# Feed-forward up-projection with the weight columns moving through TensorE, its result turned by VectorE and DRAM, its operand sums on GpSimd

## The chip, the cores and the metric

The kernel runs on one core of a Trainium2 chip. The metric is device microseconds for one execution, as the median of several runs. A core has TensorE (matmuls, "PE" in the profile, with "PEld" for its weight loads), VectorE ("DVE"), ScalarE ("ACT"), GpSimd ("POOL") and SyncE ("SP", which here only issues DMAs). The engines work at the same time, each through its own instructions in order, and wait for one another by semaphores.

## The reference

One residual block on x of 512 tokens by 2048, all in float32:

```python
h = rmsnorm(x); proj = h @ w_in                  # q, k, v of 8 + 8 heads, and forget gates
mixed = concat(headnorm(stick_breaking(...)), headnorm(forgetting(...)))
x = x + mixed @ w_out                            # 2048 x 2048
h2 = rmsnorm(x)
u = relu(h2 @ w_up)                              # 2048 x 8192
x = x + (u * u) @ w_down                         # 8192 x 2048
y = rmsnorm(x)
```

The change is in `h2 @ w_up`, called the first feed-forward product below; `(u * u) @ w_down` is the second.

## The kernel before

**Precision.** Every float32 operand is split into a high and a low part (`split`, lines 58 to 65): ScalarE rounds the operand to the high part (line 60), VectorE subtracts that from the operand (line 61). Each product is then three matmuls, high by high, high by low and low by high (`mm3`, lines 92 to 95).

**Seven products in place of eight.** Both feed-forward products are done in two-by-two blocks by Winograd's form of Strassen's method. The tokens' side has quarters a11, a21, a12, a22 (two halves of the contraction by two halves of 256 tokens), the weights' side b11, b12, b21, b22. Seven products are formed from sums of quarters. The sums of the tokens' side for the first product, "forms" in the code, are made once (`a_form`, lines 443 to 456), split, and stay in SBUF as `F[p]` for p = 1 to 7. The sums of the weights' side are made as the weights arrive, in place: in `Unit.product` there are four VectorE instructions for a unit, of 1024 elements in each partition (lines 542, 544, 546, 548).

**The first product before.** The 8192 columns of `w_up` are worked through in 32 units of 256 columns (`Unit`, line 516). For a unit two tiles of 1 MB are loaded on SP's queue (line 530; the pool `rw` has five buffers), and seven products are made. A product splits one quarter of the weights (1024 elements per partition) into a buffer from a ring (`hi_lo`, lines 69 to 75: three pairs of buffers in the pool `w`, and one more pair in `hx` from the end of the first unit on), and then does 8 x 3 matmuls: the weights are stationary (128 by 128), 256 tokens of `F[p]` move. The result has hidden columns in the partitions and tokens along the free axis, which is how the second product wants it. PSUM banks A, B and C hold running sums; ScalarE copies A out at three of the products (line 557), VectorE adds it to B or C (lines 563, 565, 569), and ScalarE applies relu and square (lines 570, 571).

**Forms of the hidden layer.** After every second unit the quarters of the result are turned into the seven forms of the second product (`store_form`, lines 573 to 581): for four of the seven VectorE makes a sum (lines 449 to 455), ScalarE and VectorE split into a buffer `st` (the tag `wraw` of the pool `w`, three buffers shared with others), and SP writes it to DRAM as `ufd`. They are read back as `uf` in the second product (`second`, lines 616 to 644), where 512 columns of `w_down` move and the forms are stationary.

**Order.** The program is written in order of work; a list scheduler with a cost model orders the instructions of each engine, and on the chip each engine then runs its list in order. The last two products of a unit (`old`, p = 4 and 3) are written in between those of the next unit (line 678).

Of the kernel before, what the change touches and what calls it, by code (L numbers as in the profile page):

```python
# [8 lines left out]
F32 = mybir.dt.float32  # L9
# [5 lines left out]
P = 128  # L15
NT = 512
# [19 lines left out]
def block_kernel(ctx, tc, x, g_attn, w_in, b_f, g_out_sb, g_out_fox, w_out, g_mlp, w_up, w_down, g_final, y):  # L36
# [399 lines left out]
    sm = ctx.enter_context(tc.tile_pool(name="sm", bufs=2, reuse_waits="tile"))  # L436
    xp_cm = tc.tile_pool(name="xp", bufs=1, reuse_waits="tile")
    xp = xp_cm.__enter__()
    trp_cm = tc.tile_pool(name="tr1", bufs=4, space=PSUM, reuse_waits="tile")
# [3 lines left out]
    def a_form(p, c, out, s=None):  # L443


        a11, a21, a12, a22 = (c[:, :, i, j:j + 2 * P] for i in range(2) for j in (0, 2 * P))
        s = a22 if s is None else s
        if p == 5:
            dve.tensor_tensor(s, a21, a22, op=ALU.add)
        if p == 6:  # L450
            dve.tensor_tensor(s, s, a11, op=ALU.subtract)
        if p == 7:
            dve.tensor_tensor(a21, a11, a21, op=ALU.subtract)
        if p == 3:
            dve.tensor_tensor(a12, a12, s, op=ALU.subtract)
        split(*out, {1: a11, 2: a12, 5: s, 6: s, 4: a22, 7: a21, 3: a12}[p])
# [3 lines left out]
    for n in range(4):  # L460
        ns = slice(n * NT, (n + 1) * NT)
        ps = [acc.tile([P, NT], F32, tag="acc", name="acco") for _ in range(TB)]
        x2 = xp.tile([P, TB, NT], F32, tag="x2", name="x2")
        for k0 in range(0, 2 * NH, 2):
# [6 lines left out]
            if k0 == 4:  # L471
                sp.dma_start(x2, xq[:, :, ns])
# [6 lines left out]
        hr = xp.tile([P, 2, 2, NT], F32, tag="hr", name="hr")  # L479
        for i in range(4):  # L480
            tr = trp.tile([P, NT], F32, tag="tr", name="tr1")
            for t in range(TB):
                pe.transpose(tr[:, t * P:(t + 1) * P], x2[:, t, i * P:(i + 1) * P], ident)
# [3 lines left out]
        s12 = xp.tile([P, 2, 2 * P], F32, tag="s12", name="s12")  # L487
        for p in (1, 5, 6, 2, 7, 4, 3):
            if n == 3 and p == 4:
                break  # L490
            a_form(p, hr, [f[:, 2 * n:2 * n + 2, :] for f in F[p]], s12)
        for t in range(TB):
            junk = xp.tile([P, NT], F32, tag="junk", name="junk")
            act.activation(junk, x2[:, t, :], AF.Square, accum_out=ss2[:, t, n:n + 1])
# [8 lines left out]
    ups_cm = tc.tile_pool(name="ups", bufs=2, space=PSUM, reuse_waits="tile")  # L503
    ups = ups_cm.__enter__()
    mps_cm = tc.tile_pool(name="mps", bufs=1, space=PSUM, side="right", reuse_waits="tile")
    mps = mps_cm.__enter__()
    M1 = [mps.tile([P, 2, NT], F32, name="m1_0")]
# [8 lines left out]
    class Unit:  # L516
        def __init__(self, u):
            self.u = u
            cols = slice(2 * u * P, 2 * (u + 1) * P)
            rows_ = w_up.rearrange("(a i p) f -> i p a f", i=2, p=P)  # L520
            if u == 0:

                self.b = [[wp.tile([P, KC // 2, P], F32, tag="wraw", name="wq") for _ in range(2)] for _ in range(1)]
                for j in range(2):
                    sp.dma_start(self.b[0][j], rows_[0][:, :, j * P:(j + 1) * P])
            else:
                self.b = []
            for i in range(len(self.b), 2):
                raw = rw.tile([P, KC // 2, 2 * P], F32, tag="rw", name="wu")
                sp.dma_start(raw, rows_[i][:, :, cols])  # L530
                self.b.append([raw[:, :, j * P:(j + 1) * P] for j in range(2)])
            self.A, self.B, self.C = (ups.tile([P, NT], F32, tag=c, name=f"ps{c}")[:, :2 * P] for c in "abc")

        def product(self, p):
            if p == 2:
                if self.u % 2 == 0:
                    hidden[0] = sg[0].tile([P, 2, 2, NT], F32, tag="c", name="c", bufs=2)
                self.pair = hidden[0]
                self.c = hidden[0][:, self.u % 2]
            (b11, b12), (b21, b22) = self.b  # L540
            if p == 5:
                dve.tensor_tensor(b11, b12, b11, op=ALU.subtract)
            if p == 6:
                dve.tensor_tensor(b11, b22, b11, op=ALU.subtract)
            if p == 4:
                dve.tensor_tensor(b21, b21, b11, op=ALU.subtract)
            if p == 7:
                dve.tensor_tensor(b12, b22, b12, op=ALU.subtract)
            hi, lo = (w.rearrange("p (a b) -> p a b", b=P) for w in hi_lo(2 * NT))
            split(hi, lo, {1: b11, 2: b21, 5: b11, 6: b11, 4: b21, 7: b12, 3: b22}[p])  # L550
            ps = {1: self.A, 6: self.A, 7: self.A, 4: self.A, 2: self.B, 5: self.C, 3: self.C}[p]
            for a in range(KC // 2):
                mm3(ps, hi[:, a, :], lo[:, a, :], F[p][0][:, a, :], F[p][1][:, a, :], a == 0 and p in (1, 2, 5), a == KC // 2 - 1)
            t1, t2 = slice(0, 2 * P), slice(2 * P, NT)
            if p in (1, 6, 7):
                self.m = sm.tile([P, 2 * P], F32, tag="m6" if p == 6 else "m", name=f"s{p}", bufs=2 if p == 6 else 1)
                act.copy(self.m, self.A)  # L557
                if p == 6:
                    self.m6 = self.m
                if p == 1:  # L560
                    self.m1 = self.m
            if p == 7:
                dve.tensor_tensor(self.c[:, 1, t2], self.m, self.C, op=ALU.add)
            if p == 2:
                dve.tensor_tensor(self.c[:, 0, t1], self.m1, self.B, op=ALU.add)
            if p == 4:
                act.copy(self.c[:, 0, t2], self.A)
            if p == 3:
                dve.tensor_tensor(self.c[:, 1, t1], self.m6, self.C, op=ALU.add)
                act.activation(self.c, self.c, AF.Relu)  # L570
                act.activation(self.c, self.c, AF.Square)

    def store_form(p, c, u):
        st = wp.tile([P, 2, 2, 2 * P], F32R, tag="wraw", name="st")
        a_form(p, c, (st[:, 0], st[:, 1]))
# [7 lines left out]
    def store_last(u, h):  # L583
        st = wp.tile([P, 2, NT], F32R, tag="wraw", name="su")
        split(st[:, 0], st[:, 1], hidden[0][:, u, h])
# [5 lines left out]
    UF_AT = dict(zip(ORDER, (1, 5, 6, 2, 7, 4, 3)))  # L591
    SUM_AT = dict(zip(ORDER[1:], (1, 5, 6, 2, 7, 4)))
    QUADS = [[2, 3], [4, 7]]
    M, uf = {}, {}
# [4 lines left out]
    def load_uf(p, group):  # L599
        uf[p] = form.tile([P, 2, group[1], 2 * P], F32R, tag=f"fh{UF_AT[p]}", name=f"uf{p}")  # L600
# [15 lines left out]
    def second(p, b, db, n, first):  # L616
# [10 lines left out]
        ps = M1[db] if p == 1 else dps.tile([P, 2, NT], F32, tag="dps", name="accd")  # L627
# [39 lines left out]
    hidden = {}  # L667
    todo, sg = [], []
    old = None
    for u in range(NU + 1):  # L670
        new = Unit(u) if u < NU else None
        if u == NU - 1:
            for p in ORDER:
                load_uf(p, GROUPS[0])
# [178 lines left out]
```

## Time and profile before

| | us |
|---|---|
| median of 3 runs | 2097.75 (2096.9 to 2097.83) |
| profiled execution, its own time | 2099.45 |
| its span, first to last instruction | 2097.7 |
| first matmul of the first feed-forward product | 818.9 |
| its end | 1473.5 |
| first matmul of the closing part (`last_product`) | 2039.55 |

The granted TensorE clock of the profiled execution is 0.998 over the span. The profile lists each engine's busy time; a matmul's own duration includes its way through the array, during which the next one has already started, so TensorE's pace is read from the distance of the starts. A "chain of waits" row names who waited, at which line, for whom, and for how long. A "windows" row gives the busy time of each engine in a stretch, with the number of instructions in brackets. Queues ("SPq") are the instruction streams that issue DMAs.

### The profile page before, as it was taken

How to read it: one execution, taken by the hardware profiler on the slowest of the kernel's cores; microseconds unless marked ns; L12 is line 12 of the kernel's file. 1: busy time of each engine (PE TensorE's matmuls, PEld its weight loads, DVE VectorE, ACT ScalarE, POOL GpSimd, SP SyncE). 2: the span in 40 equal slices, each digit the busy share in tenths (PEclk: the TensorE clock that was granted, in tenths of full speed). 3: DMA queues.
4: the chain of work that ended last, by engine and by line, in shares of the span. 5: the costliest groups of instructions: out<-in, count | busy, mean ns of one | idle time of the engine just before them, and what ended most of it. 6: DMA issues, size and time to landing. Idle time of an engine off the chain costs nothing.

```text
span 2097.7 us, 29846 instructions
## 1 busy us (share of the span) xinstructions
PE 2076.2 (99%) x12084; PEld 1841.3 (88%) x12084; DVE 1571.3 (75%) x1744; ACT 1034.7 (49%) x1396; POOL 50.5 (2%) x75
## 2 busy tenths in 40 slices
PE   8999999999999999999999999999999999999998
PEld 8888888888898888999999999999888888888886
DVE  5454555665677667878888888888788988888886
ACT  5333333444455564555666666566744443333433
POOL 0000000000010000000000000000000000000003
PEclk9999999999999999999999999999999999999999
DMA  6323323323223444466566566657856664664732
GB/s 185 88 81 91 81 82 79 81 81 85 77 81 110 155 147 151 123 209 192 181 213 199 171 208 206 189 184 248 299 202 263 237 227 178 242 251 139 268 113 81
DMA packets 239930, 339.68 MB, mean 162 GB/s; under 512 B 7936, under 2 KB 154416, under 8 KB 233776
## 3 DMA queue, kind: packets, MB, share of 16 engines
q1 hardware_dynamic: 238832, 335.64, 48.9%
q8 instruction: 95, 1.56, 0.3%
q10 hardware_dynamic: 960, 2.13, 0.3%
q14 instruction: 43, 0.35, 0.1%
HBM read 272.20 MB, written 65.54 MB: 161 GB/s over the span
## 4 chain that ended last, share of the span: by engine, by line
PE 58%; DVE 1%; DMA 0%; issue 0%; ACT 0%; SPq 0%; ACTq 0%
PE accd L93 8%; PE accd L95 8%; PE accd L94 8%; PE psa L93 6%; PE psa L95 6%; PE psa L94 6%; PE psc L93 3%; PE psc L95 3%; PE psc L94 3%; PE psb L95 1%; PE psb L94 1%; PE psb L93 1%; PE m L95 1%; PE m L93 1%; PE m L94 1%; PE acce L93 1%
## 5 line engine op out<-in xcount | busy, mean ns | idle before, releaser
L60 ACT CAST wh<-wu 128x1024 fp32r<-128x1024 f32 x164 | 171.0, 1048 | 135.9 <-PE psa L94 53.6
L61 DVE TENSOR_TENSOR wl<-wu,wh 128x1024 fp32r<-128x1024 f32 x164 | 199.6, 1222 | 45.7 <-ACT wh L60 45.4
L61 DVE TENSOR_TENSOR wl<-wraw,wh 128x1024 fp32r<-128x1024 f32 (+2 forms) x133 | 158.2, 1190 | 85.0 <-ACT wh L60 84.5
L93 PE MATMUL psa<-fh,wh 128*128 128x256 f32 x776 | 220.3, 284 | 0.8 <-ACT s L557 0.7
L94 PE MATMUL psa<-fl,wh 128*128 128x256 f32 x776 | 220.0, 284 | 0.9 <-DVE fl L61 0.9
L95 PE MATMUL psa<-fh,wl 128*128 128x256 f32 x776 | 219.8, 283 | 0.0
L60 ACT CAST wh<-wd 128x1024 fp32r<-128x1024 f32 (+1 forms) x136 | 134.7, 999 | 170.3 <-PE accd L95 108.8
L60 ACT CAST wh<-wraw 128x1024 fp32r<-128x1024 f32 (+2 forms) x133 | 135.4, 1019 | 156.7 <-PE accq L94 70.2
L93 PE MATMUL accq<-hH,wh 128*128 128x512 f32 x512 | 200.9, 392 | 0.0
L95 PE MATMUL accq<-hH,wl 128*128 128x512 f32 x512 | 200.5, 392 | 0.0
L94 PE MATMUL accq<-hL,wh 128*128 128x512 f32 x512 | 200.4, 391 | 0.0
L61 DVE TENSOR_TENSOR wl<-wd,wh 128x1024 fp32r<-128x1024 f32 (+1 forms) x136 | 155.6, 1154 | 41.9 <-ACT wh L60 41.5
L93 PE MATMUL accd<-wh,uf 128*128 128x512 f32 x436 | 169.7, 389 | 1.0 <-issue 1.0
L95 PE MATMUL accd<-wh,uf 128*128 128x512 f32 x436 | 169.6, 389 | 0.0
L94 PE MATMUL accd<-wl,uf 128*128 128x512 f32 x436 | 169.6, 389 | 0.0
L60 ACT CAST wx<-wd 128x1024 fp32r<-128x1024 f32 (+1 forms) x88 | 87.5, 1000 | 130.0 <-PE accd L95 78.2
L93 PEld LDWEIGHTS psa<-fh,wh 128*128 128x128 f32 x776 | 149.4, 192 | 1.2 <-ACT s L557 0.9
L94 PEld LDWEIGHTS psa<-fl,wh 128*128 128x128 f32 x776 | 149.4, 192 | 1.2 <-DVE fl L61 1.1
L95 PEld LDWEIGHTS psa<-fh,wl 128*128 128x128 f32 x776 | 149.3, 192 | 0.0
L61 DVE TENSOR_TENSOR wx<-wd,wx 128x1024 fp32r<-128x1024 f32 (+1 forms) x88 | 100.8, 1153 | 23.3 <-ACT wx L60 22.9
L94 PEld LDWEIGHTS accq<-hL,wh 128*128 128x128 f32 x512 | 96.2, 188 | 19.9 <-issue 0.5
L93 PEld LDWEIGHTS accq<-hH,wh 128*128 128x128 f32 x512 | 96.2, 188 | 19.6 <-issue 0.7
(299 smaller groups left out, 5502.1 us busy)
## 6 DMA issues: line engine op xcount, KB each, us to landing
wu<-in_w_up_dram SPq DMA_DIRECT2D x63, 1024.0 KB, 6.4
ufd<-st SPq DMA_DIRECT2D x98, 512.0 KB, 6.9
wd<-in_w_down_dram SPq DMA_DIRECT2D x48, 1024.0 KB, 6.9
wraw<-in_w_in_dram SPq DMA_DIRECT2D x84, 512.0 KB, 3.8
uf<-ufd SPq DMA_DIRECT2D x42, 1024.0 KB, 6.5
wraw<-in_w_out_dram SPq DMA_DIRECT2D x32, 512.0 KB, 3.5
wd<-in_w_down_dram SPq DMA_DIRECT2D x16, 768.0 KB, 6.2
uf<-ufd SPq DMA_DIRECT2D x14, 768.0 KB, 6.0
```

The lines of the kernel that those rows point to most:

```text
L60: ins = act.copy(hi, src)
L61: lows[0] = dve.tensor_tensor(lo, src, hi.bitcast(F32), op=ALU.subtract)
L93: pe.matmul(out, sh, mh, start=first, stop=False, skip_group_check=True)
L94: pe.matmul(out, sh, ml, start=False, stop=False, skip_group_check=True)
L95: pe.matmul(out, sl, mh, start=False, stop=last, skip_group_check=True)
```

## The change

The two operands of the first feed-forward product change places. The forms of the tokens are now stationary, and 512 weight columns move. The work goes by rounds in place of units: a round (`Round`) takes 1024 columns of `w_up` and half of the contraction, so there are 16 rounds, two for each group of 1024 columns. A product in a round has 2 splits of 1024 elements and 24 matmuls of 512 columns, the results lie with tokens in the partitions. Partial results are kept in SBUF (`c11`, `c12`, `c21`, `c22`), where ScalarE copies the first contribution and VectorE adds the others; relu and square follow in the second round of a group.

Since the second product wants hidden columns in the partitions, each quarter of the result is turned (`turned`): VectorE transposes blocks of 32 by 32, SP writes the tile to DRAM and reads it back in four DMAs with the block rows spread over the partitions. The forms of the hidden layer are then made from the turned tiles.

The sums of the weights' side (eight instructions of 1024 elements in a round) and the sums of the hidden layer's forms (`store_form`, four for each two units) are made by GpSimd instead of VectorE. The tokens' forms of the last quarter of the width (`left_forms`) are made inside the first round, whose matmuls don't read them. The ring `hi_lo` has three pairs of buffers during the first product, where it had four. The tiles have other places in SBUF and PSUM, and `turned` and the forms of the last two pairs of units come in the first two groups of the second product.

```diff
-    def a_form(p, c, out, s=None):
+    def a_form(p, quarters, out, s=None, eng=dve):
...
         if p == 5:
-            dve.tensor_tensor(s, a21, a22, op=ALU.add)
+            eng.tensor_tensor(s, a21, a22, op=ALU.add)
...
-    class Unit:
...
-            for a in range(KC // 2):
-                mm3(ps, hi[:, a, :], lo[:, a, :], F[p][0][:, a, :], F[p][1][:, a, :], a == 0 and p in (1, 2, 5), a == KC // 2 - 1)
...
+    class Round:
+        def __init__(self, r):
+            self.r = r
+            self.g, self.half = divmod(r, 2)
...
+        def product(self, p):
+            b11, b12, b21, b22 = self.b
+            src = {1: b11, 2: b21, 5: b11, 6: b11, 4: b21, 7: b12, 3: b22}[p]
+            ps = {2: B, 5: C, 3: C}.get(p, self.A)
+            for i in range(2):
+                hi, lo = (w.rearrange("p (a b) -> p a b", a=2) for w in hi_lo(2 * NT))
+                split(hi, lo, src[i])
+                for t in range(2):
+                    ts = slice(t * P, (t + 1) * P)
+                    for u in range(2):
+                        k = 4 * self.half + 2 * i + u
+                        mm3(ps[:, t, :], F[p][0][:, k, ts], F[p][1][:, k, ts], hi[:, u, :], lo[:, u, :],
+                            i + u == 0 and p in (1, 2, 5), i + u == 2)
+            for o, x, y in {1: [(b11, b12, b11)], 5: [(b11, b22, b11), (b12, b22, b12)], 6: [(b21, b21, b11)]}.get(p, []):
+                for i in range(2):
+                    pool.tensor_tensor(o[i], x[i], y[i], op=ALU.subtract)
+            o = {1: c11, 2: c11, 5: c22, 7: c22, 6: c12, 3: c12, 4: c21}[p]
+            if self.half == 0 and p in (1, 5, 6, 4):
+                act.copy(o, ps)
             else:
...
+                dve.tensor_tensor(o, o, ps, op=ALU.add)
+            if self.half == 1 and p in (2, 3, 7, 4):
+                act.activation(o, o, AF.Relu)
+                act.activation(o, o, AF.Square)
+
+    def turned(c, out):
+        ct = wp.tile([P, 4, 8, 32], F32, tag="wraw", name="ct")
+        dve.transpose(ct.rearrange("p j q c -> p q j c"), c.rearrange("p t (m j r) -> p (t m) j r", m=4, j=4))
+        d = dp.tile([P, 4, 2 * P], F32, tag="turn", name="turn", bufs=4)
+        sp.dma_start(d, ct.rearrange("p j q c -> p j (q c)"))
+        for i in range(4):
+            sp.dma_start(out[:, i * 2 * P:(i + 1) * 2 * P], d[32 * i:32 * (i + 1)].rearrange("r j x -> j r x"))
...
+    def store_form(p, a1, a2, u):
         st = wp.tile([P, 2, 2, 2 * P], F32R, tag="wraw", name="st")
-        a_form(p, c, (st[:, 0], st[:, 1]))
+        q = [by_chunk(a)[:, :, i::2, :] for i in range(2) for a in (a1, a2)]
+        a_form(p, q, [st[:, i].rearrange("p m (q c) -> p q m c", q=8) for i in range(2)], eng=pool)
...
+    for r in range(NR):
+        new = Round(r)
+        if r == NR - 1:
             b_first = load_b(GROUPS[0], 0)
+        for i, (who, p) in enumerate(((new, 1), (old, 4), (new, 5), (new, 2), (new, 6), (new, 3), (new, 7))):
             if who is None:
                 continue
             who.product(p)
```

More of the change, by code (lines that the diff above doesn't have):

```diff
@@ L502, in block_kernel @@
     rw = ctx.enter_context(tc.tile_pool(name="rw", bufs=5, side="right", reuse_waits="tile"))
[L503 to L507, printed above, removed]
+    mid2_cm = tc.tile_pool(name="mid2", bufs=1, reuse_waits="tile")
+    cs = mid2_cm.__enter__().tile([P, 2, 2, NT], F32, name="c1")
+    c11, c22 = cs[:, 0], cs[:, 1]
+    cs = mid.tile([P, 2, 2, NT], F32, tag="x", name="c2")
+    c12, c21 = cs[:, 0], cs[:, 1]
+    bank_cms = [tc.tile_pool(name=f"bank{i}", bufs=1, space=PSUM, side="right" if i < 2 else "left", reuse_waits="tile")
+                for i in range(4)]
+    M1_0, M1_1, B, C = (cm.__enter__().tile([P, 2, NT], F32, name=n) for cm, n in zip(bank_cms, ("psa", "psa", "psb", "psc")))
+    M1 = [M1_0, M1_1]
     GROUPS = [(0, 3), (3, 3)] + [(u, 4) for u in range(6, NU - 2, 4)]
@@ L573, in store_form @@
-    def store_form(p, c, u):
+                    f0 = (2 * self.g + j) * NT
+                    src = rows_[i][:, 4 * self.half:4 * self.half + 4, f0:f0 + NT]
+                    if r == 0 and i + j == 0:
+                        t_ = [wp.tile([P, 2, NT], F32, tag="wraw", name="wq") for _ in range(2)]
+                        for k in range(2):
+                            sp.dma_start(t_[k], src[:, 2 * k:2 * k + 2, :])
+                        self.b.append(t_)
+                    else:
+                        raw = rw.tile([P, 4, NT], F32, tag="rw", name="wu")
+                        sp.dma_start(raw, src)
+                        self.b.append(pieces_of(raw))
```

194 lines of the change are left out of this document (84 added, 110 removed).

## The prediction

> **What bounds the kernel now.** I read the page's busy times first, then the windows, then the starts of single matmuls. TensorE is busy for 99% of the span, and so it is in the stretch of the first feed-forward product (818.9 to 1473.5).
>
> ```profile
> PE 2076.2 (99%) x12084; PEld 1841.3 (88%) x12084; DVE 1571.3 (75%) x1744; ACT 1034.7 (49%) x1396; POOL 50.5 (2%) x75
> ```
> ```profile
> core 0: us, PE busy (x) PEld busy (x) DVE busy (x) ACT busy (x) POOL busy (x), PEclk, DMA share, GB/s
> 818.90:1473.50 654.60, 650.11 (x5382) 648.37 (x5380) 558.39 (x632) 397.15 (x535) 0.00 (x0) 1.00 0.62 197
> 1600.00:1800.00 200.00, 199.05 (x879) 164.50 (x878) 177.00 (x135) 82.85 (x84) 0.00 (x0) 1.00 0.60 220
> ```
>
> TensorE's pace is the distance of the starts, here five steps of each kind:
>
> ```profile
> 1099.79 0.28 PE L93 MATMUL psa<-fh,wh 128*128 128x256 f32 x1
> ...
> 1100.39 0.28 PE L95 MATMUL psa<-fh,wl 128*128 128x256 f32 x1
> ```
> ```profile
> 1699.71 0.39 PE L95 MATMUL accd<-wh,uf 128*128 128x512 f32 x1
> ...
> 1700.84 0.39 PE L94 MATMUL accd<-wl,uf 128*128 128x512 f32 x1
> ```
>
> A matmul with 256 moving columns takes 0.60/5 = 0.120 us, one with 512 takes 1.13/5 = 0.226, not twice as much. The first product has 32 units x 7 x 8 x 3 = 5376 of the former: 645.1 us of the 654.6. Another 18 of the second product lie in the stretch (4.1), so only 5.4 us are stalls. VectorE is 85% busy, GpSimd idle.
>
> **Matmuls.** 16 rounds x 7 x 24 = 2688 matmuls of 512 columns at 0.226 are 607.5 us, 37.6 less. This is the gain if all else stays hidden; two rounds (one group of 1024 columns, a period below) cost TensorE 336 x 0.226 = 75.9. [...]
>
> **VectorE in a period.**
>
> ```profile
> L61 DVE TENSOR_TENSOR wl<-wu,wh 128x1024 fp32r<-128x1024 f32 x164 | 199.6, 1222 | 45.7 <-ACT wh L60 45.4
> L61 DVE TENSOR_TENSOR st<-c,st 128x512 fp32r<-128x512 f32 x105 | 69.5, 686 | 21.0 <-ACT st L60 21.0
> L546 DVE TENSOR_TENSOR wu<-wu 128x1024 f32<-128x1024 f32 x31 | 37.9, 1222 | 0.6
> L644 DVE TENSOR_TENSOR m<-m,accd 128x1024 f32<-128x1024 f32 x84 | 102.2, 1216 | 11.4 <-PE accd L95 11.3
> ```
>
> 28 low parts x 1.22, 14 of 512 for the forms x 0.69, 10 additions from PSUM x 1.22 (as L644) and 4 transposes, which the trace doesn't show: 1024 elements, so taken at 1.22 as well (a reason for less is not in sight; at twice that, 4.9 more). Sum 60.9 of 75.9, or 80%, less than its 85% now: the 16 weight sums (as L546) and 8 form sums are gone. By VectorE alone the change fits.
>
> **GpSimd, and what it shares with VectorE.** The one tensor_tensor of GpSimd in the trace has 512 elements.
>
> ```profile
> L767 POOL TENSOR_TENSOR m<-m,gf x15: 1281/1295/1465, 2062.5 to 2088.4; 128x512 f32<-128x512 f32 x15
> ```
>
> Twice this for 1024 elements: 16 x 2.59 + 8 x 1.30 = 51.8 us a period, 68% of it. That fits too, if GpSimd and VectorE don't disturb each other. They do:
>
> ```profile
> 627.18 0.52 POOL L221 TENSOR_SCALAR_AFFINE_SELECT w<-w 128x384 f32<-128x384 f32 x1 [15.74 <-DVE w L272]
> ```
> ```profile
> 627.19 1.58 DVE L61 TENSOR_TENSOR wl<-wraw,wh 128x1024 fp32r<-128x1024 f32 x1
> ```
> ```profile
> 627.65 1.28 POOL L221 TENSOR_SCALAR_AFFINE_SELECT w<-w 128x128 f32<-128x128 f32 x1
> ```
> ```profile
> 2084.00 1.24 DVE L787 TENSOR_SCALAR m<-m,v 128x1024 f32<-128x1024 f32 x1
> ```
> ```profile
> 2084.92 1.47 POOL L767 TENSOR_TENSOR m<-m,gf 128x512 f32<-128x512 f32 x1 [0.23 <-ACT junk L765]
> ```
>
> The low-part subtraction of VectorE, alone 1.22, took 1.58 and ended (628.77) 1.07 after the first GpSimd operation (627.70); the second one waited for it in turn and took 1.28. At 2084 GpSimd's tensor_tensor ended (2086.39) 1.15 after VectorE's instruction (2085.24), there a scaling with one input; a subtraction beside a GpSimd tensor_tensor the trace doesn't show, and I take it to behave like these two cases. So each has something to itself for 1.07 us (1024 elements, VectorE) or 1.15 us (512, GpSimd). VectorE instructions with one input in PSUM are free of it, as L763 beside L767:
>
> ```profile
> L763 DVE TENSOR_TENSOR m<-m,acce 128x512 f32<-128x512 f32 x16 | 11.0, 686 | 12.9 <-PE acce L95 12.7
> ```
>
> [...]
>
> What the pair must do one after the other in a period: 28 x 1.07 + 14 x 0.535 = 37.5 for VectorE, 16 x 2.30 + 8 x 1.15 = 46.0 for GpSimd, together 83.5 us. TensorE needs 75.9 and takes 80.6 now (645.1/8). So the pair becomes the bound. 83.5 is the floor of a period: never idle. The ceiling: each of the 24 GpSimd instructions lets one VectorE subtraction pass, in the ratio 2:1 of weights to forms, so 46.0 + 16 x 1.07 + 8 x 0.535 = 67.4 us bring 16 of the 28 low parts, and the other 12 come at TensorE's pace (2.71 each, 12 matmuls), 32.5: 99.9. Between them: VectorE, in its fullest stretch above, was filled to 177.00/200 = 0.885 with TensorE kept fed; the pair filled as much gives 83.5/0.885 = 94.4. VectorE was not the limit there, so the pair should be fuller; I take the middle of 83.5 and 94.4, 89.
>
> The first period has no hidden forms, and its left forms (11 VectorE instructions of 0.535) bring the pair to 30.0 + 36.8 + 5.9 = 72.7, under 75.9. The stretch is then 7 x 89 + 75.9 + 4.1 = 703.0 against 654.6: +48.4.
>
> **The other edits.** The tokens' forms of the last width quarter leave the start of the stretch: up to the 5.4 us of stalls above, and the sum already counts the first period without any. Of what goes with the turn, per period 4 writes and 16 reads on SP's queue:
>
> ```profile
> L578 SPq DMA_DIRECT2D ufd<-st x96: 512/514/1605, 879.8 to 1458.7; - x96
> ```
> ```profile
> ufd<-st SPq DMA_DIRECT2D x98, 512.0 KB, 6.9
> us<-usd SPq DMA_DIRECT2D x4, 512.0 KB, 4.5
> wu<-in_w_up_dram SPq DMA_DIRECT2D x63, 1024.0 KB, 6.4
> ```
>
> 42 issues x 0.51 = 21 us of SP's 76, and 4 MB more beside some 12 (8 MB weights, 4 MB forms written) at a DMA share of 0.62: hidden. A weight load takes 6.4; b22 of a round takes the buffer that product 4 of the round before frees, some 16 us before product 6 needs a sum from it: after the load, a GpSimd sum (2.6) and a split (2.3) about 5 are left. A turn takes two ScalarE passes (2 x 1.06), a transpose 1.22, a write 6.9 and a read 4.5, together 14.7; c22's has three products (16.3) until a form reads it. It is covered by 1.6 us, and if that is gone, ScalarE's copy for the form waits with the weights' high parts queued behind it, while the ring's two spare buffers (5.4) still feed TensorE. Cost nothing, at most 2 late turns x 2 us x 7 = 28. The ring with three pairs in place of four gives up 2.7 us of lead; this is why the pair's delays reach TensorE sooner, and it is in the choice of 89. ScalarE has 28 x 1.05, 4 copies, 8 passes and 14 x 0.62, some 51 of 76: hidden. In the second product the last forms put four GpSimd sums beside a VectorE that is 0.885 busy: at most 4 x 1.15 = 4.6, hidden by the ring. Two PSUM buffers in place of four for the transposes after the output projection: under 1 us at each of four places, hidden between other matmuls.
>
> **The sum.** Profiled time 2099.45 (1.7 above the median of the runs shown) + 48.4 = 2148.
>
> **Rivals.**
> First, the pair does not bind, because the scheduler's list or its slack lets GpSimd work while VectorE adds from PSUM, transposes or waits. For it: VectorE's own list falls to 80%, and 16 us a period of it don't touch the pair. Against: 83.5 is already more than TensorE's 75.9 with every such gap used. Time: 8 x 75.9 + 4.1, with the old 5.4 of stalls, 616.7: 2062; with late turns 2062 to 2090. This ends on the other side. It decides where a period is under (654.6 - 4.1 - 75.9)/7 = 82.1, that is if the pair's holds are some 2% shorter than taken.
> Second, every GpSimd instruction is paid in full: the weight sums come late, ScalarE's next high part waits for them at the head of its queue, and the pair runs dry while TensorE waits. 7 x 99.9 + 75.9 + 4.1 = 779.3: 2224. For it: four GpSimd sums after product 5 stand in a row, with form sums between them, and ScalarE waits in order for both. Against: the weight sums have one or two products of lead.
> Third, the change does all it says but nothing comes of it: a period of 82.1, 2099. It needs gain and loss to cancel within 4 us, so little speaks for it.
>
> **How the numbers follow.** Forecast (periods of 83.5 to 94.4, 2109 to 2186): 0.50, its time 2148. Second rival (beyond 2186): 0.24. First rival: 0.22. Third: 0.04. What can be told from no change is about 0.2%, 4 us. So slower 0.74, same 0.04, faster 0.22. The range of 2070 to 2225 leaves out the lowest part of the first rival and what lies beyond the ceiling, some 0.2; the forecast's own range is 2109 to 2186.
>
> **What would show it.** Matmuls of the stretch start 0.226 apart within a product, with gaps between products; the stretch lasts about 700. The low parts of VectorE (line 61) grow from 1.22 to a mean near 1.8 and reach 3.3 singly; GpSimd's 1024-element sums last 2.4 to 3.5. TensorE's waits name VectorE's line 61, in 7 of 8 periods, not the first. The prediction is wrong if low parts stay at 1.22 beside running GpSimd sums, if GpSimd's 1024 elements take under 2.2, or if the gaps wait for DMAs of the turn.

## The result, and the profile after

The changed kernel takes 2282.36 us (median of 4 runs, 2281.08 to 2283.24) against 2097.79 for the kernel before (4 runs, 2096.9 to 2098.15): 1.0878 times the time, 95% interval 1.0864 to 1.0891. It is slower, as forecast, but by 185 us where 50 were forecast, and it lies beyond the range (2070 to 2225). The profiled execution took 2283.0, its span is 2281.3.

The first product of the feed-forward part now starts at 816.7 and ends at 1634.3: 817.6 us against 656.4 before and 703 in the forecast. (Before, its last matmul starts at 1475.3; the 1473.5 that the table of the kernel before gives, and with it the stretch of 654.6, is 1.8 too short.) The rest of the span takes 1463.7, before 1441.3. So 161 us of the loss are in the stretch and 22 outside it.

The page's busy times, the windows of the stretch and of 100 us within it, and those same 100 us in the kernel before (engines in the order PE, PEld, DVE, ACT, POOL, then the granted clock, the DMA share and GB/s):

```profile
PE 2118.1 (93%) x9396; PEld 1731.6 (76%) x9396; DVE 1683.3 (74%) x1572; ACT 1021.5 (45%) x1300; POOL 514.5 (23%) x263
```
```profile
816.70:1634.30 817.60, 688.84 (x2723) 538.53 (x2722) 660.56 (x452) 380.97 (x433) 451.69 (x183) 0.92 0.57 192
1000.00:1100.00 100.00, 81.93 (x325) 63.50 (x324) 79.43 (x54) 45.62 (x53) 57.94 (x24) 0.93 0.56 187
```
```profile
1000.00:1100.00 100.00, 100.00 (x835) 100.00 (x835) 86.06 (x101) 60.57 (x84) 0.00 (x0) 1.00 0.63 197
```

No engine is full. TensorE was at 100% of this window before and is at 82%; VectorE fell from 86% to 79%, GpSimd stands at 58%. And the clock that TensorE is granted is 0.92 over the stretch, where it was 1.00. Every engine waits for another part of the time. The groups of the page (busy and mean ns of one, then the idle time ahead of them), with ScalarE's copies for the forms in the kernel before as the last line:

```profile
L61 DVE TENSOR_TENSOR wl<-wu,wh 128x1024 fp32r<-128x1024 f32 x218 | 387.3, 1791 | 41.7 <-ACT wh L60 41.7
L574 POOL TENSOR_TENSOR wu<-wu 128x1024 f32<-128x1024 f32 x122 | 343.8, 2831 | 277.4 <-DVE wl L61 246.8
L61 DVE TENSOR_TENSOR st<-u,st 128x512 fp32r<-128x512 f32 x105 | 132.7, 1280 | 84.2 <-ACT st L60 84.1
L60 ACT CAST st<-u 128x512 fp32r<-128x512 f32 x105 | 62.8, 618 | 245.3 <-DMA u<-turn 108.2
```
```profile
L60 ACT CAST st<-c 128x512 fp32r<-128x512 f32 x105 | 62.1, 618 | 41.7 <-DMA ufd<-st 41.5
```

Two things are seen here. The low parts have grown from 1.222 to 1.791 us, those of the forms from 0.686 to 1.280, beside GpSimd sums of 2.831: the pair's hold, as predicted. And the last line of the changed kernel is the one that the prediction had at nothing: ahead of its copies for the forms ScalarE sat idle for 245.3 us, 108.2 of them until a turn came back from DRAM; before, it was 41.7 in all. How that reaches TensorE, in the timeline (start, duration, and in brackets the idle time ahead and what ended it):

```profile
1007.93 0.34 SPq L589 DMA_DIRECT2D turn<-ct  x1
...
1015.82 2.21 SPq L591 DMA_DIRECT2D u<-turn  x4
...
1018.69 1.04 SPq L589 DMA_DIRECT2D turn<-ct  x1
...
1024.93 0.62 ACT L60 CAST st<-u 128x512 fp32r<-128x512 f32 x1 [8.88 <-DMA u<-turn]
```
```profile
1026.55 0.80 PE L93 MATMUL psc<-wh,fh 128*128 128x512 f32 x1 [4.33 <-ACT wh L60]
1027.81 0.80 PE L94 MATMUL psc<-wl,fh 128*128 128x512 f32 x1 [0.46 <-DVE wl L61]
1028.40 0.63 PE L95 MATMUL psc<-wh,fl 128*128 128x512 f32 x1
1028.83 0.63 PE L93 MATMUL psc<-wh,fh 128*128 128x512 f32 x1
...
1031.93 0.40 PE L95 MATMUL psc<-wh,fl 128*128 128x512 f32 x1
1032.17 0.40 PE L93 MATMUL psb<-wh,fh 128*128 128x512 f32 x1
```

The write is issued at 1007.93, its reads at 1015.82, ScalarE's copy starts at 1024.93, 17.0 us after the write. ScalarE has been idle for 8.88 us, with the high part of the next weights behind that copy; TensorE stands for 4.33 us and waits for it. And then, when it has its data, it starts a matmul only every 0.43 us (1028.40, 1028.83) and not every 0.23 (1031.93, 1032.17): by the trace's clock records the clock is at half until 1031.55, 5.0 us after the gap.

To see what the stretch lost, I took the distance of the starts of neighbouring matmuls. A step above 0.30 us is a wait, counted with its excess over 0.227 and put to the line of the matmul that came late (93 needs the high part, from ScalarE; 94 the low part, from VectorE); a step of 0.40 to 0.47 is a matmul at half clock. For the stretch of 817.6 this gives: line 94 99.9 us, line 93 46.8, line 95 12.8, half clock 39.5 (198 matmuls), together 199.0. What is left is 618.6, about the time of the stretch's 2723 matmuls (2688, 19 of the second product and 16 that transpose) at 0.227 each, and near the 616.7 that the prediction had for a stretch in which the pair doesn't bind.

### The profile page after: what moved, and what is told of

Read it like the earlier page. It is cut to its first block, busy times and chain, and to the rows that moved or that the text cites. A ratio compares the mean times of both kernels' runs of the same rounds, so it can differ in the third digit from the quotient of the medians.

```text
span 2281.3 us, 24712 instructions
## 1 busy us (share of the span) xinstructions
PE 2118.1 (93%) x9396; PEld 1731.6 (76%) x9396; DVE 1683.3 (74%) x1572; ACT 1021.5 (45%) x1300; POOL 514.5 (23%) x263
## 4 chain that ended last, share of the span: by engine, by line
PE 67%; DMA 13%; DVE 11%; issue 4%; ACT 2%; SPq 1%; ACTq 0%; DVEq 0%
DVE wl L61 5%; PE accq L93 5%; PE accq L95 5%; PE accq L94 5%; DMA turn<-ct 5%; DMA u<-turn 4%; PE psc L94 4%; PE psc L95 4%; PE psc L93 4%; PE psb L94 3%; PE psb L95 3%; PE psb L93 3%; DVE st L61 3%; PE psa L94 3%; PE psa L95 3%
## 5 line engine op out<-in xcount | busy, mean ns | idle before, releaser
L61 DVE TENSOR_TENSOR wl<-wu,wh 128x1024 fp32r<-128x1024 f32 x218 | 387.3, 1791 | 41.7 <-ACT wh L60 41.7
L574 POOL TENSOR_TENSOR wu<-wu 128x1024 f32<-128x1024 f32 x122 | 343.8, 2831 | 277.4 <-DVE wl L61 246.8
L94 PE MATMUL psa<-wl,fh 128*128 128x512 f32 x512 | 215.3, 420 | 54.3 <-DVE wl L61 54.2
L93 PE MATMUL psa<-wh,fh 128*128 128x512 f32 x512 | 207.8, 408 | 14.4 <-ACT wh L60 14.4
L95 PE MATMUL psa<-wh,fl 128*128 128x512 f32 x512 | 209.3, 409 | 0.0
L61 DVE TENSOR_TENSOR wl<-wd,wh 128x1024 fp32r<-128x1024 f32 (+1 forms) x144 | 169.6, 1188 | 42.1 <-ACT wh L60 41.8
L61 DVE TENSOR_TENSOR st<-u,st 128x512 fp32r<-128x512 f32 x105 | 132.7, 1280 | 84.2 <-ACT st L60 84.1
L94 PEld LDWEIGHTS psa<-wl,fh 128*128 128x128 f32 x512 | 102.0, 199 | 93.4 <-DVE wl L61 72.6
L60 ACT CAST st<-u 128x512 fp32r<-128x512 f32 x105 | 62.8, 618 | 245.3 <-DMA u<-turn 108.2
L93 PE MATMUL psc<-wh,fh 128*128 128x512 f32 x256 | 109.3, 427 | 29.3 <-ACT wh L60 29.3
L93 PEld LDWEIGHTS psa<-wh,fh 128*128 128x128 f32 x512 | 101.5, 198 | 39.8 <-ACT wh L60 17.4
L94 PE MATMUL psc<-wl,fh 128*128 128x512 f32 x256 | 110.5, 432 | 20.0 <-DVE wl L61 20.0
```

The source lines that it names most:

```text
L60: ins = act.copy(hi, src)
L61: lows[0] = dve.tensor_tensor(lo, src, hi.bitcast(F32), op=ALU.subtract)
L93: pe.matmul(out, sh, mh, start=first, stop=False, skip_group_check=True)
L94: pe.matmul(out, sh, ml, start=False, stop=False, skip_group_check=True)
L95: pe.matmul(out, sl, mh, start=False, stop=last, skip_group_check=True)
L574: pool.tensor_tensor(o[i], x[i], y[i], op=ALU.subtract)
```

## The experiments

Each was measured once, with a profile; the kernel before, beside them, took 2097.52 to 2098.99. "Stretch" is from the first to the last matmul of the first feed-forward product; the last columns are the same sums over steps as above.

| run | us | stretch | line 93 | line 94 | half clock |
|---|---|---|---|---|---|
| before | 2097.8 | 656.4 | | | |
| after | 2282.4 | 817.6 | 46.8 | 99.9 | 39.5 |
| no sums | 2193.2 | 732.9 | 50.5 | 31.8 | 27.9 |
| no passage through DRAM | 2244.0 | 785.4 | 7.7 | 123.9 | 23.3 |
| neither | 2069.7 | 616.7 | 0.2 | 1.1 | 0 |
| sums on VectorE | 2233.4 | 766.3 | 89.0 | 32.0 | 22.4 |
| sums nobody reads, no DRAM | 2208.8 | 750.8 | 0.3 | 97.2 | 24.2 |
| only c22 through DRAM, no sums | 2117.6 | 658.8 | 20.0 | 10.8 | 10.2 |
| only c21, no sums | 2122.6 | 662.0 | 22.7 | 8.6 | 12.9 |
| only c12, no sums | 2088.3 | 630.7 | 0.9 | 11.1 | 0 |
| only c11, no sums | 2074.7 | 623.1 | 0.2 | 5.4 | 1.8 |
| no sums, reads on GpSimd's queue | 2157.0 | 694.7 | 29.5 | 27.7 | 15.8 |
| order of turns | 2255.1 | 793.7 | 21.8 | 104.7 | 35.9 |
| sums on VectorE, turns on GpSimd's queue | 2228.5 | 751.0 | 68.3 | 36.7 | 21.6 |
| the same, order of turns | 2181.8 | 716.4 | 33.4 | 39.0 | 18.7 |
| sums shared out, order of turns | 2211.9 | 744.5 | 29.1 | 65.1 | 24.1 |
| the same, forms later | 2214.2 | 747.0 | 27.1 | 71.0 | 23.4 |

Of the expectations below, several were missed: without sums (2193, between its two ranges), without DRAM (2244, just above 2240), only c12 (2088, between), only c21 (2123, above 2115), without sums with the reads on GpSimd's queue (2157, between), and the order of turns with GpSimd's queue (2182, above 2130). Sums on VectorE (2233) and, with them, the turns on GpSimd's queue (2228) came out on the side that makes the way of the turn itself the cause, though neither run takes that way out.

### One part of the change at a time

Two theories stood against each other: GpSimd's sums hold VectorE up (the prediction), or the turns come late. So each was taken out by itself, then both.

Without the sums:

```diff
-            for o, x, y in {1: [(b11, b12, b11)], 5: [...], 6: [...]}.get(p, []):
-                for i in range(2):
-                    pool.tensor_tensor(o[i], x[i], y[i], op=ALU.subtract)
...
-        a_form(p, q, [...], eng=pool)
+        split(*[...], {1: q[0], 2: q[2], 5: q[3], 6: q[3], 4: q[3], 7: q[1], 3: q[2]}[p])
```

> Leaves out every sum on GpSimd (those of the weights' side and those of the hidden layer's forms), so products and forms use the plain quarters; the turn through DRAM stays. In the changed kernel's trace the steps between TensorE's starts that are longer than 0.227 add up to some 200 us in the stretch of the first product: about 100 ahead of a matmul that needs a low part from VectorE, 47 ahead of one that needs a high part from ScalarE, 40 in matmuls at half the clock. If the exclusion between GpSimd and VectorE is the main cause, low parts go back to 1.22 us, and the span falls from 2281 by 100 to 150, to 2130 to 2180, what is left being the turn. If the turn is the main cause, the span falls by 50 at most, to 2230 or more, and ScalarE still waits some 100 us for the turn's reads.

Without the passage through DRAM:

```diff
-        ct = wp.tile([P, 4, 8, 32], F32, tag="wraw", name="ct")
-        dve.transpose(ct.rearrange("p j q c -> p q j c"), c.rearrange(...))
-        d = dp.tile([P, 4, 2 * P], F32, tag="turn", name="turn", bufs=4)
-        sp.dma_start(d, ...)
-        for i in range(4):
-            sp.dma_start(out[:, i * 2 * P:(i + 1) * 2 * P], ...)
+        dve.transpose(out.rearrange("p (j q c) -> p q j c", j=4, q=8), c.rearrange(...))
```

> Leaves out the way through DRAM: VectorE's 32 by 32 transpose writes straight into the tile that the forms are made from (so rows stay in the wrong partitions); the sums stay on GpSimd. If the exclusion is the main cause, the gaps ahead of low parts stay (about 100 us) and the span falls by 40 to 70, to 2210 to 2240. If the turn is the main cause, the span falls by 120 or more, to 2160 or less.

Both edits together, so that the matmuls, the splits, the additions from PSUM and the transposes stay:

> Leaves out both the GpSimd sums and the way through DRAM. All theories say that TensorE then sets the pace: the stretch of the first product lasts 612 to 620 us and the span is 2055 to 2075. If something else in the change costs time (the ring with three pairs of buffers, the additions from PSUM), the span stays above 2085.

And the whole computation with the sums moved to VectorE (`pool` becomes `dve` in the sums and in `a_form`):

> All sums on VectorE in place of GpSimd, nothing left out. No exclusion is left, but VectorE's own list becomes 56 + 16 x 1.13 + 8 x 0.60 = 79 us a period against TensorE's 76. If the exclusion is the main cause, the period is 82 to 90 (VectorE full, late turns added) and the span 2110 to 2180. If the turn is the main cause, the period stays near 100 and the span above 2230.

With neither, the stretch is 616.7 us long and TensorE doesn't wait. In the windows of 900 to 1500 it is full at a clock of 1.00, without both:

```profile
900.00:1500.00 600.00, 597.12 (x2626) 493.50 (x2625) 461.80 (x445) 382.71 (x436) 0.00 (x0) 1.00 0.65 222
```

So what is left of the change, the moving of 512 columns above all, gains 39.7 us of stretch (656.4 - 616.7), where the prediction had worked out 37.6, and the kernel gains 28 of it. The sums then cost 168.7 us of stretch (785.4 - 616.7), the turns 116.2 (732.9 - 616.7), and both together 200.9, not the 284.9 of their sum: the waits cover each other in part (while TensorE waits for a low part, a turn has time to come back; that reading fits, but no run tests it by itself). Both theories hold, and either alone is enough for a slower kernel.

Without the sums, the waits between 900 and 1500 (us in total, times, longest) are ScalarE's for the turn, and TensorE's for the high part behind it:

```profile
ACT st L60 <- DMA u<-turn: 78.2, 15, 6.5
...
PE psa L93 <- ACT wh L60: 28.5, 7, 5.9
```

Sums on VectorE give 2233.4: 49 less than on GpSimd, though VectorE then has 24 more instructions a period; its low parts are back at 1.215. Still the turns are waited for.

### Does the hold cost the time, or the wait for a late sum?

GpSimd's sums stay, in number and size, but work on data after its last use, so that no split or form waits for them; no passage through DRAM. The forms' sums are moved behind their last use in the same way:

```diff
-            for o, x, y in {1: [(b11, b12, b11)], 5: [...], 6: [...]}.get(p, []):
+            for o in {6: [b11], 3: [b22, b22], 7: [b22]}.get(p, []):
                 for i in range(2):
-                    pool.tensor_tensor(o[i], x[i], y[i], op=ALU.subtract)
+                    pool.tensor_tensor(o[i], o[i], o[1 - i], op=ALU.subtract)
...
```

> No passage through DRAM. The same number of GpSimd additions of the same sizes in every round, but on data after its last use, so that nobody waits for their results; the sums themselves are left out, so the result is not the reference's. If GpSimd and VectorE exclude each other in SBUF (the prediction's reason), the low parts stay at a mean of 1.6 to 2.0 us and the time stays at 2190 to 2245, near the 2244 with real sums; if the price of the sums is that the next high part and low part wait for a late result, the time falls to 2070 to 2100, as without sums (2070).

The hold it is: 134.1 of the 168.7 us remain (750.8 - 616.7), and the low parts are at 2.003 us, where they are at 1.217 with neither sums nor DRAM. What the two engines contend for, no run shows. The other 34.6 come only when somebody reads the sums. The windows and the groups of the run whose sums nobody reads, and after them those of the run with real sums (both without DRAM):

```profile
900.00:1500.00 600.00, 530.94 (x2150) 412.13 (x2151) 560.77 (x366) 312.48 (x356) 387.10 (x154) 0.96 0.50 172
```
```profile
L61 DVE TENSOR_TENSOR wl<-wu,wh 128x1024 fp32r<-128x1024 f32 x181 | 359.5, 2003 | 21.6 <-ACT wh L60 20.6
...
L61 DVE TENSOR_TENSOR st<-u,st 128x512 fp32r<-128x512 f32 x95 | 114.3, 1220 | 15.2 <-ACT st L60 15.2
```
```profile
900.00:1500.00 600.00, 510.93 (x2065) 397.62 (x2064) 559.76 (x344) 298.45 (x335) 387.08 (x148) 0.96 0.48 161
```
```profile
L61 DVE TENSOR_TENSOR wl<-wu,wh 128x1024 fp32r<-128x1024 f32 x172 | 330.4, 1945 | 3.9 <-ACT wh L60 3.9
...
L61 DVE TENSOR_TENSOR st<-u,st 128x512 fp32r<-128x512 f32 x85 | 143.7, 1703 | 19.6 <-ACT st L60 19.6
```

VectorE is busy for 93% in both (560.77 and 559.76 of 600). That is the point that the prediction's sum missed: VectorE's list is 60.9 us a period at its own durations, and what it waits for GpSimd within an instruction comes on top. With the measured means that is 60.9 + 28 x (2.003 - 1.222) + 14 x (1.220 - 0.686) = 90.2. A period, taken from the first matmul of product 2 to that of two rounds later, lasts 93.3 (92.7 to 94.3, the six in the middle of the stretch). With real sums the list is 60.9 + 28 x (1.945 - 1.222) + 14 x (1.703 - 0.686) = 95.4, of a period of 97.9 (97.0 to 98.9). By these sums VectorE's list fills 0.97 of both; the windows count the overlap of neighbouring instructions once and show 0.93. In these two runs VectorE is the bound. With the turns as well, in the changed kernel, it is busy for 0.80 of the same window and the period is 102.5: there it waits for ScalarE's copies (80.2 us for those of the forms, between 900 and 1600).

### The way through DRAM: one turn by itself

The prediction had reckoned a turn at 14.7 us against a cover of 16.3. In the trace of the changed kernel up to three turns follow each other on SP's queue: a write waits behind the reads of the turn ahead (of the tile transposed from 1013.78 to 1015.01 the write is issued at 1018.69, behind four reads from 1015.82 on and a weight load). So the theory was that a single turn is covered, and the row is what costs. Without sums, one of the four turns of a period goes through DRAM, the other three are written straight to their place:

```diff
     def turned(c, out):
+        if c is not c22:
+            return dve.transpose(out.rearrange("p (j q c) -> p q j c", j=4, q=8), c.rearrange(...))
```

> No sums on GpSimd or anywhere, and of the four turns of a period only c22's goes through DRAM; the other three are written straight to where the forms read them, so the result is not the reference's. If a single turn is covered by its products, as the prediction reckoned (14.7 against 16.3 us), and the cost comes from three turns in a row, the time is 2070 to 2085, as with no turn through DRAM at all (2070). If one turn alone is already too long, its share of the 123 us that the four cost shows: 2100 to 2140.

and the same with c12, c21 and c11 in the condition:

> No sums; of the four turns only c12's goes through DRAM, the other three are written straight, so the result is not the reference's. c22's alone cost 42 us of stretch, all four 116. If what the other three add comes from standing in a row, c12 alone, which ends a product earlier than c22 and is read at the same place, costs under 10 us: 2070 to 2080. If each turn is too long by itself, 2095 to 2115.

> No sums; only c21's turn goes through DRAM, the other three are written straight, so the result is not the reference's. It has no other turn near it in the whole kernel either, so standing in a row can't be its cost: if it is covered, 2070 to 2080; if it takes a share of what the three others add (74 us), 2095 to 2115.

> No sums; only c11's turn goes through DRAM, the other three are written straight, so the result is not the reference's. Its first reader comes more than a round later (about 40 us): 2070 to 2075 whatever the theory of the row says; if it costs more, what it costs is not a wait for its data but its place in SP's queue.

Over the stretch of 616.7 without any turn in DRAM, c22 costs 42.1 us, c21 45.3, c12 14.0 and c11 6.4. Their sum is 107.8, the four together cost 116.2. So the row, which I had held for the cause, isn't needed to explain most of the cost: turns are too long one by one, two of them by much, at 6.0 and 6.5 us a period. That doesn't price the row at 8 us: the waits of several turns can cover each other, and the runs with another queue or order, below, gain 15 to 38. And c11's 6.4 isn't a share of each period. Nobody waits for its turn; it is one wait of TensorE at the end of the stretch (5.0 us, at 1435.6), behind a VectorE that waits 4.1 for a load of `w_down`, which goes through the same queue as the turn. The timeline of the run with c22 alone, from the addition that completes it to the copy that reads it (where lines are left out of a kernel, the numbers behind them are smaller: L578 and L579 are here the two passes of ReLU and square, L588 and L590 the write and the reads of a turn):

```profile
1136.55 1.21 DVE L576 TENSOR_TENSOR c<-c,psa 128x1024 f32<-128x1024 f32 x1
...
1137.80 1.06 ACT L578 ACTIVATE c<-c 128x1024 f32<-128x1024 f32 x1 [0.47 <-DVE c L576]
1138.99 1.06 ACT L60 CAST wh<-wu 128x1024 fp32r<-128x1024 f32 x1
1139.95 1.05 ACT L579 ACTIVATE c<-c 128x1024 f32<-128x1024 f32 x1
...
1141.22 1.24 DVE L586 STREAM_TRANSPOSE ct<-c 128x1024 f32<-128x1024 f32 x1
...
1142.49 0.34 SPq L588 DMA_DIRECT2D turn<-ct  x1
```
```profile
1148.90 2.29 SPq L590 DMA_DIRECT2D u<-turn  x4
...
1150.47 1.03 ACT L60 CAST wh<-wu 128x1024 fp32r<-128x1024 f32 x1
...
1156.91 1.66 ACT L60 CAST st<-u 128x512 fp32r<-128x512 f32 x3 [5.41 <-DMA u<-turn]
...
1160.48 0.51 PE L93 MATMUL psa<-wh,fh 128*128 128x512 f32 x1 [2.48 <-ACT wh L60]
```

From 1137.76 to 1156.91 it takes 19.15 us, not 14.7. The two passes of ScalarE with a high part between them take 3.46 to the transpose (2.1 taken), the transpose 1.24 (1.22 taken), the write lands 6.4 after its issue (6.9 taken), and from the first read's issue to the copy it is 8.0: four reads, issued over 2.29 us one behind the other, where one landing of 4.5 was taken. Other traffic doesn't hold these reads: their 512 packets of 1 KB run from 1150.3 to 1156.5, and from 1150 to 1156 the DMA engines are busy for a share of only 0.24, at 81 GB/s. Why they move so slowly no run tests. The write's packets, on the other hand, start only at 1146.1; ahead of them the share is 0.95 (1142.5 to 1146.5), with transfers issued earlier. The cover is smaller too: ScalarE, which works ahead of TensorE, is through with its last high part at 1151.50, 13.7 after the addition, and stands for 5.41 us with the next one behind it. TensorE stands for 2.48 of them, then for a low part, then comes half clock: over the stretch 20.0 + 10.8 + 10.2 + 2.3 (line 95), 43 in all.

c21 alone, in its own run, takes longer still from the write to the copy, 16.6 us:

```profile
992.39 0.34 SPq L588 DMA_DIRECT2D turn<-ct  x1
994.95 0.38 SPq L555 DMA_DIRECT2D wu<-in_w_up_dram  x1
995.55 0.52 SPq L601 DMA_DIRECT2D ufd<-st  x1
996.17 4.58 SPq L590 DMA_DIRECT2D u<-turn  x4
...
1008.99 1.66 ACT L60 CAST st<-u 128x512 fp32r<-128x512 f32 x3 [6.25 <-DMA u<-turn]
```

Here the reads are issued behind a 1 MB weight load (994.95) and the write of a form. The write's last packet ends at 995.5, but the reads' packets run only from 1001.8 to 1008.4; until they start (996.2 to 1001.9) the DMA share is 0.91. So what stands between a turn's write and its reads on the queue is part of its price.

### The queue and the order of the turns

Reads on GpSimd's DMA queue, writes on SP's, no sums:

```diff
-            sp.dma_start(out[:, i * 2 * P:(i + 1) * 2 * P], ...)
+            pool.dma_start(out[:, i * 2 * P:(i + 1) * 2 * P], ...)
```

> No sums, four turns through DRAM as in the run with 2193, but the reads are issued on GpSimd's queue, which has nothing else to do; the writes stay on SP's, which no read holds any more. The sums are left out, so the result is not the reference's. If the reads that wait for their write on SP's queue are what makes the turns serial, the writes go out as soon as they are transposed and the time falls to 2090 to 2140; if the way itself is too long, it stays above 2170.

Then write and reads on GpSimd's queue in the whole computation with the sums on VectorE; the turns in another order with the sums on GpSimd; and both:

```diff
                 if i == 5:
-                    turned(c11, X)
                     turned(c12, H[:, 0])
                 if i == 6:
                     turned(c22, H[:, 1])
+                    turned(c11, X)
```

> All sums on VectorE as in the run with 2233, and the turn's write and its four reads issued on GpSimd's DMA queue in place of SP's, in the same order of turns. If the turn costs because a read that waits for its write holds SP's queue (the next turn's write and the weights behind it), the stretch falls from 766 to about 650 to 700 and the time to 2110 to 2165. The turns still stand in a row on one queue, so a part stays. If the way to DRAM and back costs by its own length, the time stays above 2210.

> The change with its turns in another order (the hidden forms' c22 turned before c11, so that the form that reads c22 first has a product more); the sums stay on GpSimd. If the turns cost because three follow each other on SP's queue and the one needed first is not the one sent first, the stretch of the first product falls by 20 to 60 us and the time to 2220 to 2260. If the hold between GpSimd and VectorE is what bounds the stretch and the turn's waits lie beside it, the time stays within 10 us of 2282.

> As the run with the turn on GpSimd's DMA queue, and c22 turned before c11. If the serial turns are the cause, this gives most of what is left: 2080 to 2130, below the run with the queue alone by 20 us or more. If the order does nothing once SP's queue is free, it is within 10 us of that run.

The order is worth 24 us of stretch with the sums on GpSimd (817.6 to 793.7) and 35 with the sums on VectorE (751.0 to 716.4): c12 and c22 are read first, and c11, which alone costs 6.4, no longer goes ahead of them. The queue alone is worth 15 (766.3 to 751.0) with the sums on VectorE, where write and reads change queue, and 38 without sums (732.9 to 694.7), where the reads alone do. In that last run ScalarE waits no less for the turns:

```profile
ACT st L60 <- DMA u<-turn: 107.6, 21, 8.6
...
PE psc L93 <- ACT wh L60: 18.9, 7, 3.6
```

107.6 us, against 78.2 with the reads on SP, yet TensorE loses less behind them. The expectation (2090 to 2140) was missed at 2157. Why freeing SP's queue helps TensorE while ScalarE's wait grows, these runs don't settle; other transfers pass through that queue as well.

### Sharing the sums out, and making the forms later

b11's sum and those of the forms on VectorE, those of b12 and b21 on GpSimd, with the order of turns above:

```diff
-                    pool.tensor_tensor(o[i], x[i], y[i], op=ALU.subtract)
+                    (dve if o is b11 else pool).tensor_tensor(o[i], x[i], y[i], op=ALU.subtract)
```

> The whole computation. The sums are shared out: b11's and the forms' on VectorE, those of b12 and b21 on GpSimd (8 of the 16 weight sums of a period), and c22 is turned before c11. By the hold between the two engines the pair then needs 37.5 + 8 x 1.07 + 8 x 0.535 + 8 x 2.30 = 68.7 of 75.9 us and VectorE 75: the low parts' mean falls to 1.4 to 1.6, and the stretch to 700 to 740, the time to 2150 to 2195, where all on GpSimd gave 2255 and all on VectorE 2182 with this order of turns. If sharing out gains nothing over the ends, it is within 10 us of 2182 or above.

Besides, the forms of the even rounds one product later in the program:

```diff
-            if r > 1 and i > 1:
-                k = (i - 2) * 2
+            if r > 1 and i > 1 + (new.half == 0):
+                k = (i - 2 - (new.half == 0)) * 2
...
-                    if i == 5:
+                    if i == 6:
                         turned(c21, H[:, 0])
```

> The whole computation, as the run with the shared-out sums and c22 turned before c11; besides, in the even rounds the forms that read c12 and c22 are made one product later (about 8 us). If the turns cost because they are late by some 5 to 12 us against the copy that reads them, most of their wait goes: 2110 to 2150, 30 us or more below the run without the shift. If their wait was hidden beside the pair's, it is within 10 us of it.

Shared out, the time is 2211.9: 43 better than all on GpSimd with that order, but above the 2150 to 2195 expected; the low parts still take 1.516. Its turns are on SP's queue, so it has no partner that differs in the sums alone among the runs with the sums on VectorE; that sharing is worse than 2181.8 is not shown. The later forms did nothing (2214.2), but in that trace ScalarE's copies still follow the turns as closely as before: the forms begin 14 us after the transpose, 1018.7 after 1004.9, with 1021.8 after 1007.9 without the edit. The scheduler put them back where they had been. So the run says nothing of the cover.

No version with the whole computation beats the kernel before. The best, 2181.8, is 84 above it: sums on VectorE make its list 86 us a period (60.9 + 16 x 1.22 + 8 x 0.69), more than the 80.6 that TensorE took for the same work before.

## Why the prediction was wrong

The sign was right, the size was not: 2148 forecast, 2282 measured. By its steps:

- **Matmuls.** Right: 37.6 us forecast, 39.7 measured without sums and DRAM, stalls included. That the first rival's stretch of 616.7 was met to the tenth is luck: its 5.4 us of stalls come from the end at 1473.5; to 1475.3 the kernel before has 7.2 (656.4 - 645.1 - 4.1).
- **The hold of VectorE and GpSimd.** The hold was there, as forecast: low parts at a mean of 1.791 (near 1.8 forecast), GpSimd's sums at 2.831 (2.4 to 3.5 forecast), and it remains when nobody reads the sums (low parts at 2.003, in place of 1.222 before the change). The prediction had taken it from two cases with other instructions; the run with unread sums shows it for the subtraction beside a GpSimd tensor_tensor. The size of the hold failed at the step "I take the middle of 83.5 and 94.4, 89". The pair was treated as one resource that can be filled while VectorE does its other 16 us. But while VectorE waits inside a low part it does nothing else, so the list of VectorE is what has to be summed, with its waits: 90 to 95 us, filled to 0.97. The period is 93.3 with the hold alone, within the forecast's own 83.5 to 94.4, and 97.9 with real sums, nearer to the second rival's ceiling of 99.9, in place of 89; about 3 us of each are half clock. A second step failed with it: the first period, taken at TensorE's pace as its sum was only 72.7, isn't spared. From the stretch's start to product 2 of the third round the run without DRAM takes 108.0, the one with unread sums 101.6, that with neither 89.3. So some 19 and 12 us were lost where nothing was taken. In the stretch: 750.8 and 785.4 in place of 703.
- **The turn.** This is the step that failed in kind: "Cost nothing, at most 2 late turns x 2 us x 7 = 28". Two late turns there are, c22 and c21, but at 6.0 and 6.5 us a period, and c12 adds 2.0; without the sums the four cost 116, on top of the sums 32 (817.6 - 785.4). The working named the mechanism (the copy waits, the high parts are queued behind it) and mis-sized both sides of it: 14.7 for a way that took 19.15, mostly four reads of 1 KB pieces counted as one landing, and 16.3 for a cover that ScalarE uses up in 13.7. From the write's issue to the first copy alone it is 14.4 us for c22 and 16.6 for c21, where 11.4 was taken.
- **The clock.** Not in the prediction at all. Half clock after gaps takes 39.5 us of the stretch.
- **Outside the stretch** 22 us were lost, where at most 4.6 and four times under 1 us were taken. In the run without sums and DRAM the rest of the span is 1451.2; so 12 of the 22 hang on the change's sums and turns. The other 10 weren't looked into further.
- Of what was to show it, the mean of the low parts and GpSimd's durations came as forecast; the waits for line 61 came in the first period too, and "if the gaps wait for DMAs of the turn" came as the sign against it. Whether a fourth pair in the ring, as before, would have hidden part of either wait, no run tests.

The kind of error is the same in the two large terms: two rows were set against each other as sums of durations (14.7 against 16.3, 83.5 against 75.9), where what counts is an engine that takes its work in order and does nothing else while it waits.

## What to carry to other kernels

Where two engines hold each other up, as VectorE and GpSimd do here (low parts of 2.003 us in place of 1.222), add the waits to the list of the engine that has other work too, and compare that list with the bound; a shared resource's own fill is only a floor (83.5 us reckoned, a period of 93.3 measured). A round trip through DRAM is priced from the trace as the way from the write's issue to the first reader (14 to 17 us here for 0.5 MB), with every read DMA of it, and its cover is counted up to where the reading engine's queue gets to the reader, not to where the bound engine needs it. An in-order engine that feeds the bound engine should not be the first reader of a late transfer: what stands behind it, stands (8.88 us of ScalarE's idling and 4.33 of TensorE's in the timeline above).

## What the runs showed of the hardware that was not expected

Short gaps of TensorE cost more here than their length. In the kernel before, half clock took 3.4 us of the stretch; in the changed one 126 us, by the clock records of the two traces in pieces of 3.41 or 6.83 us and one of 10.24, mostly behind gaps of 2 to 5 us. A matmul then takes 0.43 us in place of 0.23, and 198 such matmuls lose 39.5 us. The length of a gap alone doesn't tell whether half clock follows: in the changed kernel it followed three gaps of 2.17 us (ahead of 973.18, 1280.61 and 1382.58) and one of 2.21 (ahead of 1177.42), but not three others of 2.21 (ahead of 1076.27, 1486.47 and 1588.53).

A single turn cost TensorE more than the wait for it: in the period shown of the run with c22 alone 5.41 us of ScalarE's idling became 2.48 of TensorE's, and with the next low part and the half clock behind it a period was 6.0 us longer in the mean.
